# Cross-covariance attention: V and output in 2 KB runs, attention doubled by a selector matmul, and a new order of the loop

## The chip, the cores and the metric

The kernel runs on one core of one Trainium2 chip. The metric is the device time in microseconds (us) of one execution. Most executions of a kernel agree within about a per cent. For a program on one core, a run over 1.5% above the fastest of its kernel counts as slow. The engines are PE (matmul), DVE (vector), ACT (scalar), POOL and SP (which issues the DMAs).

## The reference

Q, K and V are float32 of shape (8, 12, 512, 64): 96 heads of 512 rows and 64 columns.

```python
Q_norm = Q / (np.linalg.norm(Q, axis=-2, keepdims=True) + 1e-10)
K_norm = K / (np.linalg.norm(K, axis=-2, keepdims=True) + 1e-10)
attn = np.einsum('bhnd,bhne->bhde', Q_norm, K_norm)          # 64 x 64 per head
attn = np.exp(attn - np.max(attn, axis=-1, keepdims=True))
attn = attn / (np.sum(attn, axis=-1, keepdims=True) + 1e-10)
return np.einsum('bhnd,bhde->bhne', V, attn).astype(np.float32)
```

Attention is between columns, so the only large work is to move 3 x 12.6 MB in and 12.6 MB out.

## The kernel before

A unit `u` is four heads; there are 24. All loads give each of the 128 partitions four consecutive rows of a head, so one contiguous run in memory is 4 x 64 x 4 B = 1 KB. The parts that matter (cuts marked):

```python
Vf = V.rearrange("b h (p t) d -> p (b h) t d", p=128)       # Q, K and out alike: 1 KB runs
...
def casts(u):       # DVE: four casts of Q and K to bf16, one of V
    ...
def grams(u):       # PE: 16 matmuls, [Q|K]^T [Q|K] of four heads
    ...
def norms(u):       # DVE: the squared norms from the grams' diagonals; POOL: power -0.5
    ...
def scale_k(u):     # DVE: kqs = gram * rk, masked
    ...
def logits(u):      # PE: kqs^T * stacked identities (needs scale_k)
    ...
def exps(u):        # ACT: exp with the scale rq, and row sums
    ...
def normalise(u):   # DVE: ab = exp / sum, written block-diagonally, two heads per 128 x 128
    ...
def vtrans(u):      # PE transposes V, ACT copies it out
    ...
def outs(u):        # PE: 8 matmuls of 128 x 128 x 128; ACT copies and reorders
    ...
for s in range(U + 2):
    ...                        # load unit s + 3, store unit s - 6
    if s < U:
        grams(s)
        norms(s)
    if 0 <= s - 1 < U:
        logits(s - 1)
        exps(s - 1)
    if s < U:
        vtrans(s)
    if s + CAST_AHEAD < U:
        casts(s + CAST_AHEAD)  # CAST_AHEAD = 1
    if 0 <= s - 1 < U:
        normalise(s - 1)
    if s < U:
        scale_k(s)
    if 0 <= s - 2 < U:
        outs(s - 2)
```

The loop is a software pipeline. The order written here is the order in which each engine executes; the trace shows it of PE, for one (`gram` at 71.00 us, `lg` 73.63, `vps` 74.54, `po` 75.39).

## Time and profile before

145.01 us, median of 3 runs (144.89 to 145.13).

| | before |
|---|---|
| profile's span | 143.1 us |
| busy: PE, DVE, ACT | 95.3, 100.9, 64.8 us |
| DMA packets of the data queue, their share of 16 engines | 50,688; 104.5% |
| mean granted clock of PE | 0.74 of full |

Lines of the page of the kernel before. The digits of `DMA` are tenths of busy share in 40 equal slices of the span, `GB/s` the rate in each; `q1` is the data queue (packets, MB, share of 16 engines' span); the last line is the chain of waits by engine. `PEld` is PE's loading of weights, `SPq` and the like are an engine's sequencer, which issues its instructions and DMAs, and `issue` is time for which the profile shows no wait.

```profile
span 143.1 us, 2715 instructions
...
PE 95.3 (67%) x864; PEld 83.7 (59%) x864; DVE 100.9 (71%) x432; ACT 64.8 (45%) x193; POOL 29.9 (21%) x39
...
DMA  4999999999999999999999999999999999999993
GB/s 133 336 353 349 348 348 351 350 348 348 348 350 348 376 370 378 368 371 384 368 372 380 372 376 379 371 380 371 375 369 369 371 382 372 382 377 386 377 322 113
...
q1 hardware_dynamic: 50688, 50.34, 104.5%
...
DMA 65%; DVE 14%; SPq 12%; PE 2%; ACT 1%; issue 1%; ACTq 0%
```

DMA is busy in every slice, its engines' time is used up (packet times that add up to 104.5% of the 16 engines' span: some packets of one engine must overlap in the records), and most of the chain of waits is DMA. No compute engine is above 71%. The kernel is bound by DMA, first at about 350 GB/s (loads alone), then at about 375 (loads and stores).

The groups (busy us and mean ns of one after the first bar; idle time just before them, and what ended it, after the second):

```profile
L84 DVE CAST vb<-vf 128x1024 bf16<-128x1024 f32 x24 | 16.7, 694 | 15.2 <-DMA vf<-in_V_dram 15.2
...
L100 DVE CUSTOM_DVE_ANT_0 scr<-gram,swap 128x128 f32<-128x128 f32 x48 | 13.7, 286 | 0.0
L100 DVE CUSTOM_DVE_ANT_0 scr<-gram,ident 128x128 f32<-128x128 f32 x48 | 13.6, 284 | 0.0
```

DVE waits for V's DMA, but never for PE ahead of the norms (`scr`): their idle time is 0.0.

One unit of the timeline (start us, us, engine, line, operation; in brackets the idle time before it and what ended it):

```profile
76.59 1.89 PE L92 MATMUL gram<-qkb 128*128 128x128 bf16 x16
77.47 0.69 DVE L84 CAST vb<-vf 128x1024 bf16<-128x1024 f32 x1 [0.60 <-DMA vf<-in_V_dram]
...
78.08 0.16 DVE L131 RECIPROCAL rinv<-esum 128x2 f32<-128x2 f32 x1
78.27 0.61 DVE L134 SCALAR_TENSOR_TENSOR ab<-ex,rinv,blocks 128x128 bf16<-128x128 f32 x2
78.80 0.60 DVE L111 SCALAR_TENSOR_TENSOR kqs<-gram,rq,blocks 128x128 f32<-128x128 f32 x2
...
79.20 1.12 PE L119 MATMUL lg<-eye,kqs 128*128 128x64 f32 x4 [0.73 <-DVE kqs L111]
79.32 0.28 DVE L100 CUSTOM_DVE_ANT_0 scr<-gram,ident 128x128 f32<-128x128 f32 x1
```

The grams of this unit start before V is even there to be cast, and end about when DVE comes to its multiplies, so that DVE runs casts, reciprocal, `ab`, `kqs` and the norms in one piece. `logits` (`lg`) run beside the norms. A unit takes about 5.55 us here, and DVE works about 4.2 of them.

### The profile page before, as it was taken

To read this page: it belongs to the slowest core of one execution; us is meant where nothing else is said; L and a number is where in the kernel's file an instruction comes from. 1 tells how busy PE (TensorE), PEld (TensorE's weight loads), DVE (VectorE), ACT (ScalarE), POOL (GpSimd) and SP (SyncE) were. 2 spreads that over 40 slices of the span, in tenths; PEclk is the share of its full clock that TensorE was granted. 3 is DMA by queue.
4 is the path that set the end of the run, shared out by engine and by line. 5 is a ranking of instruction groups with operands and counts; after the bars stand their busy time and mean duration, and the time that the engine had idled before them with its cause. 6 is when DMAs were issued, how large, how long until landed. Compare 5 with 4: busy or idle time off the path is not lost.

```text
span 143.1 us, 2715 instructions
## 1 busy us (share of the span) xinstructions
PE 95.3 (67%) x864; PEld 83.7 (59%) x864; DVE 100.9 (71%) x432; ACT 64.8 (45%) x193; POOL 29.9 (21%) x39
## 2 busy tenths in 40 slices
PE   0245879775896797686559874776795694397820
PEld 0234669664795686575557763765694683397620
DVE  0435888989888987696786886883868868767410
ACT  3003406764377644715706536437074273371840
POOL 6003302332033330311302303302022032031100
PEclk9999999999559856857975589655559559855555
DMA  4999999999999999999999999999999999999993
GB/s 133 336 353 349 348 348 351 350 348 348 348 350 348 376 370 378 368 371 384 368 372 380 372 376 379 371 380 371 375 369 369 371 382 372 382 377 386 377 322 113
DMA packets 50701, 50.49 MB, mean 353 GB/s; under 512 B 1536, under 2 KB 50688, under 8 KB 50688
## 3 DMA queue, kind: packets, MB, share of 16 engines
q1 hardware_dynamic: 50688, 50.34, 104.5%
q8 instruction: 6, 0.10, 0.3%
q14 instruction: 7, 0.06, 0.1%
HBM read 37.75 MB, written 12.58 MB: 352 GB/s over the span
## 4 chain that ended last, share of the span: by engine, by line
DMA 65%; DVE 14%; SPq 12%; PE 2%; ACT 1%; issue 1%; ACTq 0%
DMA vf<-in_V_dram 59%; DMA qf<-in_Q_dram 6%; SPq L65 5%; DVE vb L84 4%; SPq L66 4%; DVE ab L134 4%; SPq L70 3%; DVE scr L100 3%; DVE kqs L111 2%; PE lg L119 2%; ACT ex L125 1%; DVE rinv L131 1%; PE po L153 0%; ACT so L154 0%; DVE qkb L78 0%
## 5 line engine op out<-in xcount | busy, mean ns | idle before, releaser
L92 PE MATMUL gram<-qkb 128*128 128x128 bf16 x384 | 39.6, 283 | 20.0 <-DVE qkb L80 19.4
L105 POOL TENSOR_TENSOR rq<-nsq,mhalf 128x4 f32<-128x4 f32 x24 | 27.6, 1151 | 102.0 <-DVE nsq L100 102.0
L92 PEld LDWEIGHTS <-qkb 128*128 128x128 bf16 x384 | 33.8, 130 | 25.3 <-DVE qkb L80 24.6
L125 ACT ACTIVATE ex<-lg,rq 128x64 f32<-128x64 f32 x48 | 14.7, 310 | 63.2 <-PE lg L119 63.2
L119 PE MATMUL lg<-eye,kqs 128*128 128x64 f32 x96 | 22.8, 381 | 19.4 <-DVE kqs L111 19.3
L119 PEld LDWEIGHTS lg<-eye,kqs 128*128 128x128 f32 x96 | 18.8, 271 | 24.9 <-DVE kqs L111 24.9
L145 ACT COPY vt<-vps 128x512 bf16<-128x512 bf16 x48 | 25.7, 593 | 8.7 <-PE vps L143 8.7
L84 DVE CAST vb<-vf 128x1024 bf16<-128x1024 f32 x24 | 16.7, 694 | 15.2 <-DMA vf<-in_V_dram 15.2
L154 ACT COPY so<-po 128x512 f32<-128x512 f32 x48 | 26.4, 618 | 0.3 <-PE po L153 0.3
L143 PE MATMUL vps<-identb,vb 128*128 128x128 bf16 x192 | 20.9, 274 | 1.9 <-DVE vb L84 1.9
L153 PE MATMUL po<-ab,vt 128*128 128x128 bf16 x192 | 20.9, 274 | 0.6 <-DVE ab L134 0.6
L143 PEld LDWEIGHTS <-vb 128*128 128x128 bf16 x192 | 19.3, 138 | 2.2 <-DVE vb L84 2.2
L80 DVE CAST qkb<-kf 128x512 bf16<-128x512 f32 x24 | 10.2, 424 | 11.6 <-DMA kf<-in_K_dram 11.6
L153 PEld LDWEIGHTS <-vt 128*128 128x128 bf16 x192 | 17.4, 129 | 0.9 <-DVE ab L134 0.9
L134 DVE SCALAR_TENSOR_TENSOR ab<-ex,rinv,blocks 128x128 bf16<-128x128 f32 x48 | 14.7, 349 | 0.9
L111 DVE SCALAR_TENSOR_TENSOR kqs<-gram,rq,blocks 128x128 f32<-128x128 f32 x48 | 14.5, 344 | 0.0
L78 DVE CAST qkb<-qf 128x512 bf16<-128x512 f32 x24 | 10.2, 425 | 5.1 <-DMA qf<-in_Q_dram 5.1
L100 DVE CUSTOM_DVE_ANT_0 scr<-gram,swap 128x128 f32<-128x128 f32 x48 | 13.7, 286 | 0.0
L100 DVE CUSTOM_DVE_ANT_0 scr<-gram,ident 128x128 f32<-128x128 f32 x48 | 13.6, 284 | 0.0
L79 DVE CAST qkb<-qf 128x512 bf16<-128x512 f32 x24 | 10.1, 420 | 0.0
L81 DVE CAST qkb<-kf 128x512 bf16<-128x512 f32 x24 | 10.1, 419 | 0.0
L125 ACT ACTIVATION_READ_ACCUMULATOR ex<-lg,rq 128x1 f32 x48 | 9.4, 196 | 0.0
(18 smaller groups left out, 15.8 us busy)
## 6 DMA issues: line engine op xcount, KB each, us to landing
qf<-in_Q_dram SPq DMA_DIRECT2D x24, 512.0 KB, 8.3
kf<-in_K_dram SPq DMA_DIRECT2D x24, 512.0 KB, 8.4
vf<-in_V_dram SPq DMA_DIRECT2D x24, 512.0 KB, 8.4
out_dram<-so SPq DMA_DIRECT2D x24, 512.0 KB, 7.9
```

The costliest lines, as they stand in the source:

```text
L84: nc.vector.tensor_copy(w.rearrange("p t h d -> p h t d"), vf[u])
L92: nc.tensor.matmul(o, x, x, start=(t == 0), stop=(t == T - 1))
L100: nc.vector.tensor_tensor_reduce(out=scr, in0=blk, in1=m, scale=1.0, scalar=1e-20, op0=ALU.mult, op1=ALU.add, accum_out=n2[:, c, p:p + 1],)
L105: nc.gpsimd.tensor_tensor(out=r, in0=n2, in1=mhalf, op=ALU.pow)
L111: nc.vector.scalar_tensor_tensor(out=kk[:, p], in0=gram[u][:, p, 0::3, :], scalar=rq[u][:, 1, p:p + 1], in1=off_diag, op0=ALU.mult, op1=AL ...
L119: nc.tensor.matmul(l[:, p, :], kqs[u][:, p].rearrange("p a d -> p (a d)"), eye2)
L125: nc.scalar.activation(e[:, p, :], lg[u][:, p, :], AF.Exp, scale=rq[u][:, 0, p:p + 1], accum_out=s[:, p:p + 1])
L134: nc.vector.scalar_tensor_tensor(out=a[:, p], in0=e[:, p, None, :].to_broadcast([128, 2, D]), scalar=ri[:, p:p + 1], in1=on_diag, op0=ALU. ...
L143: nc.tensor.transpose(ps[:, t, :], vb[u][:, t, 2 * p:2 * p + 2, :].rearrange("p h d -> p (h d)"), identb)
L145: nc.scalar.copy(w, ps)
L153: nc.tensor.matmul(po[:, t], vt[u, p][:, t, :], ab[u][:, p].rearrange("p a d -> p (a d)"))
L154: nc.scalar.copy(s[:, 2 * p:2 * p + 2].rearrange("p h t d -> p t h d"), po)
```

## The change

The intent is that 2 KB runs for V and the output cost DMA less per byte. A partition then holds eight consecutive rows of V, 64 partitions make a head, and two heads lie side by side on the partitions. Row pairs are transposed (128 x 128: two rows of 64 columns), so the attention of a head is needed on both halves of the partitions, block-diagonally. A selector matmul (`pick`) doubles it, and two ACT copies place the blocks. The output matmuls become 64 columns wide and stand in pairs on the two column halves of PE. The order of the loop changes too.

```diff
-    Vf = V.rearrange("b h (p t) d -> p (b h) t d", p=128)
-    Of = out.rearrange("b h (p t) d -> p (b h) t d", p=128)
+    Vf = V.rearrange("b h n d -> (b h n d)").rearrange("(s p f) -> p s f", p=128, f=RV * D)
+    Of = out.rearrange("b h n d -> (b h n d)").rearrange("(s p f) -> p s f", p=128, f=RV * D)
@@ normalise
-            nc.vector.scalar_tensor_tensor(          # 128 x 128, with the block mask
-                out=a[:, p], in0=e[:, p, None, :].to_broadcast([128, 2, D]), ...
+            nc.vector.tensor_scalar_mul(a[:, p, :], e[:, p, :], ri[:, p:p + 1])     # 128 x 64
+    def doubled(u):
+        d = ps_d.tile([128, 2, PU, D], F32, name="dup")
+        for c in range(2):
+            nc.tensor.matmul(d[:, c], pick[:, c, :], at[u])
+        a = ab[u] = abuf[u % len(abuf)]
+        nc.scalar.copy(a[0:D, :, :, 0, :], d[0:D].rearrange("p c u d -> p u c d"))
+        nc.scalar.copy(a[D:, :, :, 1, :], d[D:].rearrange("p c u d -> p u c d"))
@@ outs
-                nc.tensor.matmul(po[:, t], vt[u, p][:, t, :], ab[u][:, p].rearrange("p a d -> p (a d)"))
+                for x in range(HS):
+                    nc.tensor.matmul(po[NV * x:NV * (x + 1), k, :], vt[u][:, g, t, NV * x:NV * (x + 1)],
+                        ab[u][:, h // 2, h % 2].rearrange("p a d -> p (a d)"), tile_position=(0, NV * x))
@@ the loop
-        if s < U:
-            grams(s)
-            norms(s)
         if 0 <= s - 1 < U:
             logits(s - 1)
             exps(s - 1)
         if s < U:
+            grams(s)
+            norms(s)
             vtrans(s)
 ...
         if 0 <= s - 2 < U:
             outs(s - 2)
+        if 0 <= s - 1 < U:
+            doubled(s - 1)
```

Left out: one vt copy of 1024 columns for two of 512, the constants, the pools' sizes.

More of the change, by code (lines that the diff above doesn't have):

```diff
@@ L17 @@
 PU = HU // 2
+RV = 8
+NV = 512 // RV
+HS = 128 // NV
+SV = HU // HS
+TP = RV // 2
 @with_exitstack
@@ L47 @@
     qkp = ctx.enter_context(tc.tile_pool(name="qkp", bufs=4))
-    vtp = ctx.enter_context(tc.tile_pool(name="vtp", bufs=4))
+    vtp = ctx.enter_context(tc.tile_pool(name="vtp", bufs=3))
     sop = ctx.enter_context(tc.tile_pool(name="sop", bufs=10))
@@ L52 @@
     ps_v = ctx.enter_context(tc.tile_pool(name="ps_v", bufs=2, space=bass.MemoryType.PSUM))
-    ps_l = ctx.enter_context(tc.tile_pool(name="ps_l", bufs=2, space=bass.MemoryType.PSUM))
+    ps_l = ctx.enter_context(tc.tile_pool(name="ps_l", bufs=1, space=bass.MemoryType.PSUM))
+    ps_d = ctx.enter_context(tc.tile_pool(name="ps_d", bufs=1, space=bass.MemoryType.PSUM))
     ps_o = ctx.enter_context(tc.tile_pool(name="ps_o", bufs=2, space=bass.MemoryType.PSUM))
@@ L58 @@
     STORE_LAG = 6
-    qf, kf, vf, vb, qkb, gram, nsq, kqs, rq, lg, ex, ab, vt, so = ({} for _ in range(14))
+    qf, kf, vf, vb, qkb, gram, nsq, kqs, rq, lg, ex, at, ab, vt, so = ({} for _ in range(15))
     def load_qk(u):
@@ L68, in load_v @@
     def load_v(u):
-        vf[u] = vp.tile([128, HU, T, D], F32, name="vf")
-        nc.sync.dma_start(out=vf[u], in_=Vf[:, u * HU:(u + 1) * HU])
+        vf[u] = vp.tile([128, SV, RV * D], F32, name="vf")
+        nc.sync.dma_start(out=vf[u], in_=Vf[:, u * SV:(u + 1) * SV])
     def store(u):
-        nc.sync.dma_start(out=Of[:, u * HU:(u + 1) * HU], in_=so[u])
+        nc.sync.dma_start(out=Of[:, u * SV:(u + 1) * SV], in_=so[u])
     def casts(u):
@@ L81, in casts @@
         nc.vector.tensor_copy(t_[:, 1::2, :, 0:D], kf[u][:, 1::2])
-        w = vb[u] = vbp.tile([128, T, HU, D], BF16, name="vb")
-        nc.vector.tensor_copy(w.rearrange("p t h d -> p h t d"), vf[u])
+        w = vb[u] = vbp.tile([128, SV, TP, 2 * D], BF16, name="vb")
+        nc.vector.tensor_copy(w.rearrange("p s t d -> p s (t d)"), vf[u])
     def grams(u):
@@ L131, in normalise @@
         nc.vector.reciprocal(ri, s)
-        a = ab[u] = small.tile([128, PU, 2, D], BF16, name="ab")
+        a = at[u] = small.tile([128, PU, D], BF16, name="at")
         for p in range(PU):
-            nc.vector.scalar_tensor_tensor(
-                out=a[:, p], in0=e[:, p, None, :].to_broadcast([128, 2, D]), scalar=ri[:, p:p + 1], in1=on_diag,
-                op0=ALU.mult, op1=ALU.mult,
-            )
-    def vtrans(u):
-        for p in range(PU):
-            ps = ps_v.tile([128, T, 128], BF16, name="vps")
-            for t in range(T):
-                nc.tensor.transpose(ps[:, t, :], vb[u][:, t, 2 * p:2 * p + 2, :].rearrange("p h d -> p (h d)"), identb)
-            w = vtp.tile([128, T, 128], BF16, name=f"vt{p}")
-            nc.scalar.copy(w, ps)
-            vt[u, p] = w
@@ L148, in outs @@
-    def outs(u):
-        s = so[u] = sop.tile([128, HU, T, D], F32, name="so")
-        for p in range(PU):
-            po = ps_o.tile([128, T, 2, D], F32, name="po")
-            for t in range(T):
-                nc.tensor.matmul(po[:, t], vt[u, p][:, t, :], ab[u][:, p].rearrange("p a d -> p (a d)"))
-            nc.scalar.copy(s[:, 2 * p:2 * p + 2].rearrange("p h t d -> p t h d"), po)
+            nc.vector.tensor_scalar_mul(a[:, p, :], e[:, p, :], ri[:, p:p + 1])
[6 more added lines that the diff above has]
+        nc.scalar.copy(a[D:, :, :, 1, :], d[D:].rearrange("p c u d -> p u c d"))
@@ new lines, in vtrans @@
+    def vtrans(u):
+        ps = ps_v.tile([128, SV, TP, 128], BF16, name="vps")
+        for g in range(SV):
+            for t in range(TP):
+                nc.tensor.transpose(ps[:, g, t, :], vb[u][:, g, t, :], identb)
+        w = vt[u] = vtp.tile([128, SV, TP, 128], BF16, name="vt")
+        nc.scalar.copy(w, ps)
+    def outs(u):
+        s = so[u] = sop.tile([128, SV, TP, 2 * D], F32, name="so")
+        for i in range(2):
+            po = ps_o.tile([128, 4, 2 * D], F32, name="po")
+            for k in range(4):
+                g, t = divmod(4 * i + k, TP)
+                for x in range(HS):
+                    h = g * HS + x
+                    nc.tensor.matmul(
+                        po[NV * x:NV * (x + 1), k, :], vt[u][:, g, t, NV * x:NV * (x + 1)],
+                        ab[u][:, h // 2, h % 2].rearrange("p a d -> p (a d)"), tile_position=(0, NV * x),
+                    )
+            nc.scalar.copy(s.rearrange("p g t d -> p (g t) d")[:, 4 * i:4 * i + 4, :], po)
@@ L171 @@
     nc.gpsimd.tensor_tensor(out=eye2, in0=ident[:, :D], in1=ident[:, D:], op=ALU.add)
-    blocks = const.tile([128, 3, D], F32, name="blocks")
-    nc.gpsimd.memset(blocks, 0.0)
-    nc.gpsimd.memset(blocks[0:D, 1, :], 1.0)
-    nc.gpsimd.memset(blocks[D:, 0, :], 1.0)
-    nc.gpsimd.memset(blocks[D:, 2, :], 1.0)
-    off_diag = blocks[:, 0:2, :]
-    on_diag = blocks[:, 1:3, :]
+    off_diag = const.tile([128, 2, D], F32, name="off_diag")
+    nc.gpsimd.memset(off_diag, 0.0)
+    nc.gpsimd.memset(off_diag[0:D, 1, :], 1.0)
+    nc.gpsimd.memset(off_diag[D:, 0, :], 1.0)
+    pick = const.tile([128, 2, 128], BF16, name="pick")
+    for c in range(2):
+        for i in range(2):
+            nc.gpsimd.tensor_copy(pick[:, c, i * D:(i + 1) * D], ident[:, c * D:(c + 1) * D])
+    abuf = []
+    for i in range(3):
+        a = const.tile([128, PU, 2, 2, D], BF16, name=f"ab{i}")
+        nc.gpsimd.memset(a, 0.0)
+        abuf.append(a)
     mhalf = const.tile([128, 2, PU], F32, name="mhalf")
```

## The prediction

> **What bounds the kernel now.** DMA. The page's slice rows show DMA busy above 90% in all but the end slices, at 350 to 380 GB/s; 50,688 packets take 104.5% of the 16 engines' span, so a 1 KB packet costs about 48 ns of one engine. The chain of waits is 65% DMA (vf loads 59%). No compute engine is full: DVE 100.9 us of 143.1, PE 95.3, ACT 64.8. In steady state one unit (4 heads, 2 MB) takes about 5.55 us (timeline, 69 to 83 us); DVE works about 4.2 of these.
>
> **What the change does.**
> - DMA: V and output go from 1 KB to 2 KB runs, 512 packets fewer per unit. [...]
> - DVE: two 128x128 ab multiplies (pair 0.53 us) become two 128x64 ones (estimate 0.35). Casts unchanged. About 3.95 us per unit.
> - ACT: one 1024-wide vt copy for two of 512 (about equal), plus two half-partition copies (about 0.8 us): about 3.5 us per unit, not limiting.
> - PE: output matmuls 8 to 16 per unit, plus 2 selector matmuls: 1 us more per unit.
> - Order: logits(s-1) now stands ahead of grams(s). This decides it.
>
> **Critical path.** DVE issues kqs(s-1), then at once norms(s). Before, grams(s) had run earlier, during the V cast, and norms followed without a gap (DVE idle before norms: 0.0 in the groups). Now kqs(s-1) -> logits(s-1) -> grams(s) -> norms(s) is serial: PE waits for kqs, then runs both, while DVE stands idle. [...] Lengths from the timeline:
> - kqs start to logits start 0.40; to the next matmul 0.53 at full clock (29.0 us), 0.91 at half (14.9 us); 16 grams 1.18 or 1.89; to DVE about 0.1
> - norms to casts 0.92; casts 1.36; V cast 0.61; reciprocal 0.20; multiplies 0.35, then kqs
>
> Sum: 5.65 us per unit at full clock, 6.74 at half. [...]
>
> Clock: in the trace, stretches at half clock with PE busy over about 95% are followed by full clock, those at full clock below about 57% by half. The new loop leaves PE a gap of 1.7 us per unit at full clock, 0.7 at half, so it should toggle, about half each: 6.15 us. First kqs at 14.3, 23 units, then 9 us of tail: 14.3 + 141.5 + 9 = 165; profile span and measured time differ by about 2. All at full clock: 155; all at half: 180.
>
> **Predicted: 165 us, 155 to 175; faster 0.03, same 0.04, slower 0.93.**
>
> **What would show it.** DMA share falls to about 85%, mean GB/s to about 310. DVE idle ahead of its norms line, released by PE gram, 1.7 to 2.8 us per unit (40 to 65 in all). The chain of waits turns from DMA to DVE and PE lines. V and output packets halve and land no slower. DVE's waits for DMA nearly vanish.
>
> **What would make it wrong.** A clock that stays full or half throughout. Column-tiled output matmuls that stall PE beyond its gap (slower still). Casts or norms shorter than the timeline shows, so that DMA still bounds[...].

The sum is whole: 14.3 + 23 x 6.15 + 9 = 165. The DMA share of 85% was the estimate; the kernel before's 104.5% of 143.1 us, spread over a span of 163, would be 92%. DMA does not bound: the 5.55 us per unit of the kernel before are already under 5.65. Estimates are also the 0.35 us for the multiplies and the 0.8 for the two copies; 0.43 and 0.73 (2 x 367 ns) were measured.

## The result

The changed kernel takes 169.66 us (168.46 to 171.19, 4 runs); the ratio to the kernel before is 1.167 (95% interval 1.160 to 1.175). Ratios here and below are the mean time of one kernel's fast runs over that of the other's in the same rounds, so not quite the ratio of the quoted medians. The one exception is e9, whose recorded ratio its two fast runs alone do not give (see there).

The first profile fell in the run of 171.19 us, which counts as slow (1.6% above the fastest). Run e10 below repeats the kernel, with a profile of state fast; it shows the same pieces with the same lengths, so the reading does not rest on the state.

Lines of the page of the changed kernel, same parts as before, with the chain by line as well:

```profile
span 169.1 us, 3252 instructions
...
PE 104.8 (62%) x1104; PEld 92.3 (55%) x1104; DVE 94.4 (56%) x432; ACT 83.5 (49%) x217; POOL 33.6 (20%) x45
...
DMA  4999999999999999999999999999998113033063
GB/s 173 321 372 361 360 360 361 360 360 360 368 385 388 386 386 378 390 388 391 386 391 386 358 334 300 343 311 361 343 377 342 49 75 124 14 116 124 0 241 131
...
q1 hardware_dynamic: 38400, 50.34, 85.9%
...
DVE 45%; PE 39%; DMA 6%; issue 3%; ACT 2%; SPq 1%; ACTq 0%; DVEq 0%
PE gram L98 22%; PE lg L125 13%; DVE scr L106 12%; DVE vb L90 8%; DMA vf<-in_V_dram 6%; DVE at L140 6%; PE dup L146 5%; DVE qkb L85 4%; DVE qkb L87 4%; DVE qkb L88 4%; DVE qkb L86 4%; DVE rinv L137 1%; ACT so L172 1%; SPq L73 1%; SPq L72 1%
```

The packets fell from 50,688 to 38,400 as planned, and DMA's engines have time over (85.9%). It is busy through three quarters of the span (9 in slices 2 to 30 of 40), as loads may run up to five units ahead (`vf` has five buffers): V's last load is issued at 120.5 us and its last cast begins at 153.0. Then little is left but stores. The chain of waits is now DVE and PE, in alternation. Its groups:

```profile
L106 DVE CUSTOM_DVE_ANT_0 scr<-gram,ident 128x128 f32<-128x128 f32 x48 | 13.9, 289 | 56.3 <-PE gram L98 56.3
...
L168 PE MATMUL po<-ab,vt 128*64 128x128 bf16 x384 | 19.5, 260 | 1.2 <-ACT ab L149 1.2
...
L90 DVE CAST vb<-vf 128x1024 bf16<-128x1024 f32 x24 | 16.4, 684 | 3.2 <-DMA vf<-in_V_dram 3.2
...
L106 DVE CUSTOM_DVE_ANT_0 scr<-gram,swap 128x128 f32<-128x128 f32 x48 | 13.7, 286 | 0.0
```

The first of the norms (`scr`, mask `ident`) now finds DVE idle for 56.3 us in all, ended by PE's grams; in the kernel before that was 0.0. In turn DVE's wait for V fell from 15.2 to 3.2 us.

The chain in order of time, one unit whose `lg` and grams ran at full clock and a part of one at half (start us, us, what; the repeated `scr` and the casts of Q and K are left out):

```profile
71.00 0.28 PE dup L146 x2
...
71.34 0.63 PE lg L125 x4
71.97 0.91 PE gram L98 x16
...
72.91 0.29 DVE scr L106
...
75.18 0.60 DVE vb L90
...
75.89 0.43 DVE at L140 x2
...
76.37 0.40 PE dup L146 x2
76.76 1.04 PE lg L125 x4
77.80 1.72 PE gram L98 x16
...
79.55 0.29 DVE scr L106
```

At 71.00 and again at 76.37 DVE's multiplies (`at`) release the doubling (`dup`); `kqs`, which follows `at` on DVE, releases `lg`, then come the grams, and only then DVE's `scr`. From `scr` to `scr` it is 6.64 us; that unit ran at half clock through `lg` (1.04) and grams (1.72). In the one before they took 0.63 and 0.91. (PE's granted clock is either full or half in the records of these traces, 1.0 or 0.5 in all 14 of the kernel before and all 34 of this one, nothing between; "at half clock" below is said of the stretch in question.) Over the whole trace, `kqs` starts first at 14.2 us and for the 24th time at 159.6: 23 units of 6.32 us in the mean (the shortest 5.37, eleven of them 6.64 or 6.65). Before, it was 14.5 to 133.2, 5.16 each. The heads and tails differ little (9.5 us after the last `kqs`, 9.9 before), so the 26 us of longer span are in the units: 23 x 1.16 = 26.7.

The work in a unit, in stretches of one unit each (columns as in the first line; the last three are clock, DMA share and GB/s). A unit at half clock of the kernel before:

```profile
core 0: us, PE busy (x) PEld busy (x) DVE busy (x) ACT busy (x) POOL busy (x), PEclk, DMA share, GB/s
...
77.80:83.40 5.60, 4.76 (x40) 4.23 (x38) 4.29 (x19) 2.64 (x8) 1.09 (x1) 0.50 1.08 373
```

Two units of the changed kernel. The first had full clock for `lg` and the grams and half clock later (0.71 in the mean), the second half clock throughout:

```profile
70.50:75.90 5.40, 3.65 (x46) 3.07 (x46) 3.89 (x19) 3.43 (x9) 1.21 (x1) 0.71 1.07 386
75.90:82.50 6.60, 4.99 (x46) 4.37 (x46) 3.88 (x18) 3.43 (x9) 1.21 (x1) 0.50 1.07 388
```

DVE works less than before (3.89 against 4.29 us), ACT more (3.43 against 2.64), PE a quarter of a microsecond more. None fills its unit. The time went into waiting.

### The profile page after: what moved, and what is told of

Read it like the earlier page. It is cut to its first block, busy times and chain, and to the rows that moved or that the text cites. A ratio compares the mean times of both kernels' runs of the same rounds, so it can differ in the third digit from the quotient of the medians.

```text
span 169.1 us, 3252 instructions
## 1 busy us (share of the span) xinstructions
PE 104.8 (62%) x1104; PEld 92.3 (55%) x1104; DVE 94.4 (56%) x432; ACT 83.5 (49%) x217; POOL 33.6 (20%) x45
## 2 busy tenths in 40 slices
DMA packets 38415, 50.53 MB, mean 299 GB/s; under 512 B 1536, under 2 KB 26112, under 8 KB 38400
## 3 DMA queue, kind: packets, MB, share of 16 engines
q1 hardware_dynamic: 38400, 50.34, 85.9%
## 4 chain that ended last, share of the span: by engine, by line
DVE 45%; PE 39%; DMA 6%; issue 3%; ACT 2%; SPq 1%; ACTq 0%; DVEq 0%
PE gram L98 22%; PE lg L125 13%; DVE scr L106 12%; DVE vb L90 8%; DMA vf<-in_V_dram 6%; DVE at L140 6%; PE dup L146 5%; DVE qkb L85 4%; DVE qkb L87 4%; DVE qkb L88 4%; DVE qkb L86 4%; DVE rinv L137 1%; ACT so L172 1%; SPq L73 1%; SPq L72 1%
## 5 line engine op out<-in xcount | busy, mean ns | idle before, releaser
L158 ACT COPY vt<-vps 128x1024 bf16<-128x1024 bf16 x24 | 24.3, 1012 | 46.9 <-PE vps L156 44.9
L106 DVE CUSTOM_DVE_ANT_0 scr<-gram,ident 128x128 f32<-128x128 f32 x48 | 13.9, 289 | 56.3 <-PE gram L98 56.3
L98 PEld LDWEIGHTS <-qkb 128*128 128x128 bf16 x384 | 41.0, 148 | 6.3 <-DVE qkb L87 6.3
L146 PE MATMUL dup<-at,pick 128*128 128x128 bf16 x48 | 7.7, 249 | 45.2 <-DVE at L140 45.1
L148 ACT CAST ab<-dup 64x256 bf16<-64x256 f32 x24 | 8.8, 367 | 24.1 <-PE dup L146 24.1
L168 PE MATMUL po<-ab,vt 128*64 128x128 bf16 x384 | 19.5, 260 | 1.2 <-ACT ab L149 1.2
L168 PEld LDWEIGHTS <-vt 128*64 128x64 bf16 x384 | 15.1, 134 | 4.8 <-issue 3.8
L117 DVE SCALAR_TENSOR_TENSOR kqs<-gram,rq,off_diag 128x128 f32<-128x128 f32 x48 | 14.5, 344 | 0.7 <-POOL rq L111 0.7
L85 DVE CAST qkb<-qf 128x512 bf16<-128x512 f32 x24 | 10.7, 445 | 4.4 <-DMA qf<-in_Q_dram 4.4
L87 DVE CAST qkb<-kf 128x512 bf16<-128x512 f32 x24 | 10.0, 418 | 0.9 <-DMA kf<-in_K_dram 0.9
L140 DVE TENSOR_SCALAR at<-ex,rinv 128x64 bf16<-128x64 f32 x48 | 10.0, 251 | 0.9
```

The lines of the kernel that those rows point to most:

```text
L85: nc.vector.tensor_copy(t_[:, 0::2, :, 0:D], qf[u][:, 0::2])
L98: nc.tensor.matmul(o, x, x, start=(t == 0), stop=(t == T - 1))
L106: nc.vector.tensor_tensor_reduce(out=scr, in0=blk, in1=m, scale=1.0, scalar=1e-20, op0=ALU.mult, op1=ALU.add, accum_out=n2[:, c, p:p + 1],)
L140: nc.vector.tensor_scalar_mul(a[:, p, :], e[:, p, :], ri[:, p:p + 1])
L146: nc.tensor.matmul(d[:, c], pick[:, c, :], at[u])
L158: nc.scalar.copy(w, ps)
```

## The experiments

The theory: the new order makes `kqs(s-1)` -> `logits(s-1)` -> `grams(s)` -> `norms(s)` a serial link between DVE and PE, and the loop through it (5.37 to 6.65 us in the trace) is mostly longer than DMA's 5.4 us (2.10 MB of a unit at the 387 GB/s that e4 shows). The rival: the added work (doubling, twice the output matmuls, ACT copies) costs the time. A third question is the clock, which the link's length follows (at full and half clock `lg` took 0.63 and 1.04 us, the grams 0.91 and 1.72). The 5.3 us of DMA per unit in the expectations is the estimate; the traces give the same, 5.55 of the kernel before less the 0.24 that e4's expectation takes from the packet records. Four kernels of the first set, e1 to e4, ran on one chip beside the kernel before (144.44 us there); e5 to e8 together (144.64); e9 and e10 together (144.91).

| run | what | median us | ratio to before (95%) |
|---|---|---|---|
| e1 | changed, old order of grams and logits | 142.56 | 0.987 (0.979 to 0.994) |
| e2 | before, new order alone | 175.49 | 1.209 (1.200 to 1.219) |
| e3 | changed, old order, doubling a unit later | 141.82 | 0.979 (0.973 to 0.985) |
| e4 | before, 2 KB runs alone (wrong result) | 140.74 | 0.971 (0.965 to 0.977) |
| e5 | changed, DVE's norms behind the casts | 144.45 | 0.999 (0.996 to 1.002) |
| e6 | changed, PE kept busy | 154.21 | 1.063 (1.057 to 1.068) |
| e7 | e3, tail split over two engines | 141.38 | 0.977 (0.974 to 0.980) |
| e8 | e3 again | 141.30 | 0.978 (0.975 to 0.981) |
| e9 | changed, doubling a unit later alone | 167.99 (fast runs 166.6) | 1.160 (1.149 to 1.171) |
| e10 | changed, again | 172.20 | 1.188 (1.184 to 1.193) |

All but e4 gave a correct result.

### e1: the old order back

```diff
+        if s < U:
+            grams(s)
+            norms(s)
         if 0 <= s - 1 < U:
             logits(s - 1)
             exps(s - 1)
         if s < U:
-            grams(s)
-            norms(s)
             vtrans(s)
```

> The changed kernel with one thing undone: grams and norms of unit s again stand ahead of logits and exps of unit s-1. Order theory (the order makes a serial loop over DVE and PE): the link through logits (0.63 us at full clock, 1.04 at half, by the changed kernel's chain) leaves the loop; but the doubling of unit s-1, which waits for the multiplies late in the DVE's unit, still stands ahead of the next grams, so a part of the loop stays: DVE work 3.95 plus idle 0.9 to 1.8 us, 4.9 to 5.75 us per unit, near the 5.3 us of DMA. Expected 142 to 150 us. Rival (cost theory: the new selector matmuls, 384 instead of 192 output matmuls and the two more ScalarE copies cost the time, the order does not matter): stays at 162 or more.

Measured 142.56 us: with all the added work in place, the loss is gone. The rival falls, and with it the smaller pools of the change, which this kernel has too. The waits of this kernel (what waited for what: us in total, times, longest):

```profile
DVE scr L106 <- PE gram L98: 26.1, 22, 1.7
```

The idle time ahead of the norms has halved, not vanished: the doubling still holds the grams until the multiplies are done. The units are 4.68 us at full clock and 5.60 at half. That is near DMA's pace of 5.4 us, so little of it shows in the total.

### e2: the new order alone

```diff
-        if s < U:
-            grams(s)
-            norms(s)
         if 0 <= s - 1 < U:
             logits(s - 1)
             exps(s - 1)
         if s < U:
+            grams(s)
+            norms(s)
             vtrans(s)
```
(in the kernel before; nothing else is changed)

> The kernel before with the changed order alone (logits and exps of unit s-1 ahead of grams and norms of unit s), nothing else. Order theory: DVE work 4.2 us per unit plus idle ahead of the norms of about 1.4 (full clock) or 2.6 us (half), 5.5 to 6.8 us per unit, in all 160 to 172 us, DVE idle ahead of norms 35 to 60 us. Cost theory: about 145 us, as before.

Measured 175.49 us, above the stated range: the order alone costs more than the whole change. The idle time ahead of the norms is the changed kernel's:

```profile
PE lg L119 <- DVE kqs L111: 60.7, 24, 3.8
DVE scr L100 <- PE gram L92: 56.3, 23, 2.7
```

Two engines wait for each other in turn. Why it went over the range: its units run from 5.55 to 6.78 us, as stated, but 14 of the 23 are over 6.7, the half-clock length. I had counted on a more even mix. The clock records of this trace (from 17 us to the last `kqs`) give full clock for 37% of the time, but for only 11% of the time of `lg` and the grams; e10 shows why.

### e3: old order, and the doubling one unit later

```diff
 # on top of e1
+        if 0 <= s - 2 < U:
+            doubled(s - 2)
         if s < U:
             vtrans(s)
 ...
             outs(s - 2)
-        if 0 <= s - 1 < U:
-            doubled(s - 1)
```

> The changed kernel with the old order and the doubling one unit later (of unit s-2, after logits of s-1, so that it waits for nothing). Order theory: no PE wait is left between kqs and norms, DVE idle ahead of norms near 0, DMA bounds again at about 5.3 us per unit: 138 to 142 us, faster than the kernel before. Cost theory: 160 or more.

Measured 141.82 us, as stated. Its data queue and chain by engine:

```profile
q1 hardware_dynamic: 38400, 50.34, 101.4%
...
DMA 72%; DVE 9%; SPq 8%; ACT 3%; PE 3%; issue 1%; ACTq 0%
```

The wait of DVE for the grams in the same kernel (engine, line and tile, what it waited for: us in total, times, longest us):

```profile
DVE scr L106 <- PE gram L98: 1.0, 1, 1.0
```

DMA bounds again, with the fewer packets. This version beats both kernels, by about 2% against the kernel before.

### e4: the 2 KB runs alone

```diff
-    Vf = V.rearrange("b h (p t) d -> p (b h) t d", p=128)
-    Of = out.rearrange("b h (p t) d -> p (b h) t d", p=128)
+    Vf = V.rearrange("b h n d -> (b h n d)").rearrange("(s p f) -> p s f", p=128, f=8 * D)
+    Of = out.rearrange("b h n d -> (b h n d)").rearrange("(s p f) -> p s f", p=128, f=8 * D)
```
(in the kernel before, with the two transfers reshaped to match; the matmuls take the rows for others than they are)

> The kernel before with V read and the output written in 2 KB runs and nothing else changed; the result is wrong on purpose (rows land where the matmuls do not expect them). It measures what the 2 KB runs are worth where DMA bounds. From the traces: a 2 KB packet took 84 ns (median) where two of 1 KB took 92, so about 0.24 us per unit, 6 us in all: 138 to 141 us. If the packets' length is worth nothing because the memory bounds: 145.

Measured 140.74 us, 3.7 us less than the kernel before beside it by the medians (3.3 to 5.0 by the ratio's interval). So this is what the longer runs are worth by themselves. Rates by slice, and the queue:

```profile
GB/s 125 334 358 360 363 363 364 355 358 362 363 363 357 389 382 383 382 382 391 387 382 394 386 383 393 384 387 388 389 377 392 383 396 383 386 404 407 335 310 159
...
q1 hardware_dynamic: 38400, 50.34, 102.5%
```

Against the page of the kernel before, loads alone rise from about 350 to 360 GB/s, loads with stores from about 375 to 387. e3 with all the real work comes within 1.1 us of this.

### e5: the same PE order, another place for the norms on DVE

```diff
             grams(s)
-            norms(s)
             vtrans(s)
         if s + CAST_AHEAD < U:
             casts(s + CAST_AHEAD)
+        if s < U:
+            norms(s)
```

> The changed kernel, PE order left as it is, but on DVE the norms of unit s now stand behind the casts of unit s+1. Order theory in full (the time is lost only because DVE's very next instruction behind kqs waits for the PE link): the casts, about 1.95 us, fill the wait; the loop is kqs 0.53 + casts 1.95 (or the PE link, 2.1 to 3.3) + norms 0.84 + the POOL power 1.4 = 4.8 to 5.6 us per unit, near the 5.3 of DMA: 140 to 148 us, DVE idle ahead of norms under 20 us in all. Rival (logits ahead of grams costs PE itself the time, whatever DVE does): 162 or more.

Measured 144.45 us. PE's order is the changed kernel's, and 25 us are gone because DVE has the casts to do while PE runs the link:

```profile
DVE kqs L117 <- POOL rq L111: 18.0, 24, 1.2
...
DVE scr L106 <- PE gram L98: 7.6, 9, 2.7
```

DVE's wait for PE fell from 56.3 to 7.6 us, and a smaller one for POOL's power came in its place, 18.0 us. Neither the order on PE nor that on DVE loses the time by itself: it takes a link on PE and a DVE whose next instruction in order waits for that link.

### e6: PE kept busy in its gap

```diff
         d = ps_d.tile([128, 2, PU, D], F32, name="dup")
+        for _ in range(12):
+            nc.tensor.matmul(d[:, 0].rearrange("p u d -> p (u d)"), pick[:, 0, :], pick[:, 1, :])
         for c in range(2):
             nc.tensor.matmul(d[:, c], pick[:, c, :], at[u])
```

> The changed kernel with 12 useless 128-column matmuls ahead of each doubling, in the time in which PE waits for the multiplies (1.65 us or more per unit in the changed kernel's trace); the result is unchanged. Clock theory (the loop runs at 5.37 us per unit at full clock and at 6.64 at half, and is mostly at half because PE idles in it): [...] units 5.4 us, 14.2 + 23 x 5.4 + 9.5 + 2 = 150 us (147 to 155). Rival (the clock makes little difference, or the filler only delays): 168 or more.

Measured 154.21 us: 288 useless matmuls make the changed kernel some 15 us faster. The units are 5.37 us where the clock is full (13 of 23 within 0.02 of it), their mean 5.61. PE was busy for 67% of such a unit (3.58 of 5.37 us); in the changed kernel's one unit wholly at full clock it was 53% (2.82 of 5.37). The changed kernel's PE gaps of over 0.5 us (from 18 us to the last `kqs`) were 2.0 us in the mean, 2.6 at most; here the useless matmuls take 0.84 us of a unit at full clock and leave a gap of 1.7. From 18 us to the last `kqs` the records give full clock for 78% of the time, and for 68% of that of `lg` and the grams. The wait for the grams shrank accordingly:

```profile
DVE scr L106 <- PE gram L98: 40.0, 23, 2.7
```

Of the changed kernel's 25 us of loss, about 15 fell away with the clock (the changed kernel did not run beside this one, so the 15 is rough). The other 10 are the link at full clock, and the units that still ran slower.

### e7 and e8: a shorter tail

```diff
 # e7, on top of e3: for the last two units
+        if u >= U - 2:
+            nc.vector.tensor_copy(a[D:, :, :, 1, :], ...)   # one of the two doubling copies on DVE
+            if u >= U - 2 and i == 0:
+                nc.vector.tensor_copy(o, po)                # one of the two output copies on DVE
```

> The kernel of e3 with, in the last two units, one of the two doubling copies and one of the two output copies on DVE, which idles there. e3's chain ends 4.1 us of ScalarE and PE work after the last multiplies; about 1 us of it would fall away: 140.5 to 142 us, at most 0.7% under e3. If the end is bound by the stores' drain instead: as e3.

> e3 unchanged, beside e7 on the same chip with more rounds: a ratio of 0.975 to 0.985 to the kernel before. It tells whether e3 is faster by over 2% and whether e7 gains anything.

e8 repeats e3: 141.30 us, ratio 0.978 (0.975 to 0.981). e7's 141.38 and 0.977 are not distinct from it: inconclusive, and no gain can be claimed. Whether e3 is faster by over 2% is at the edge of the interval.

### e9: the doubling a unit later, logits still first

```diff
 # in the changed kernel
             grams(s)
             norms(s)
+        if 0 <= s - 2 < U:
+            doubled(s - 2)
+        if s < U:
             vtrans(s)
 ...
-        if 0 <= s - 1 < U:
-            doubled(s - 1)
```

> The changed kernel, logits still ahead of grams, but the doubling one unit later as in e3: the fourth corner beside the changed kernel, e1 and e3. Order theory: the link kqs - logits - grams - norms stays whole; only the doubling's 0.1 us between kqs and logits falls away, so 2 to 3 us less than the changed kernel: 164 to 169 us, DVE idle ahead of norms still over 45 us. Rival (the doubling's wait for the multiplies is what holds PE up, and e1 gained by chance of the two together): under 155.

Measured 167.99 us (the two fast runs 166.34 and 166.79). With the changed kernel (172.20 beside it), e1 and e3 this is the fourth corner. The recorded ratio of 1.160 seems to count the slow runs too: the mean of the two fast ones, 166.6, is 1.150 times that of the kernel before beside them. Fast runs against fast runs, moving the doubling is worth 5.5 us where logits stand first (2 to 3 were expected; 166.6 against 172.1) and about 1 where they do not (142.0 against 142.9); moving the logits is worth 25 us with the doubling late and 29 without, across two sessions. The rival of this run falls. The doubling's own part is small: the shortest and longest units are 5.34 and 6.58 us (5.37 and 6.64 in the changed kernel), 1.4 us at most in 23 units. The rest of the gain is that more units had full clock for their link (mean 6.07 us against 6.40 in e10).

### e10: the changed kernel again

> The changed kernel once more, beside e9 on the same chip, for a profile in the fast state (the first profile fell in a run 1.6% above the fastest). 168 to 171 us; units of 5.4 us at full clock and 6.64 at half, as in the first profile; if the slower run had another cause, the lengths of its pieces would differ from this one's.

Measured 172.20 us, just over the stated range, on another chip than e1 to e8. The profile is of a fast run of 172.05 us. PE's clock by slice, as the page has it, and the chain by engine:

```profile
PEclk9999999999999998769678555555769678587965
...
DVE 45%; PE 41%; DMA 6%; issue 2%; SPq 1%; ACT 1%; POOLq 1%; ACTq 0%; DVEq 0%
```

Its wait of DVE for the grams:

```profile
DVE scr L106 <- PE gram L98: 58.2, 23, 2.7
```

The same waits, the same pieces: its units are 6.64 us in 15 of 23, the shortest full ones 5.6. It is slower than the first profile's 171.19 because fewer units caught the full clock (mean 6.40 against 6.32), with no piece longer. In its first 15 slices the page prints a clock of 9 where the units take the half-clock 6.64 us, with the 1.65 us of idle PE that goes with half clock throughout; the trace has no clock record before 63 us there. The mean granted clock of a run (0.807 here, 0.735 in the first profile) is therefore no measure of it; the lengths of the units are.

What decides which units are caught can be read from the clock records of the traces. They change in steps of 3.41 us, so a half and a full stretch in turn last 6.83 us, and a unit 6.64. Six units in a row of the first profile (from 38.5 us) show what follows:

| half stretch begins, us after the unit's `kqs` | 0.14 | 0.33 | 0.52 | 0.73 | 1.12 | 1.89 |
|---|---|---|---|---|---|---|
| length of the unit, us | 6.64 | 6.64 | 6.62 | 6.43 | 6.06 | 5.37 |

A half stretch that begins with the link covers `lg` and the grams, and the full stretch behind it is spent largely on PE's gap. It begins 0.19 us later after each unit of 6.64 us, and more after the shorter ones, until it misses the link and a unit is short. e10 repeats this row (0.29, 0.48, 0.66, 1.01, 1.66 us; 6.64, 6.64, 6.48, 6.17, 5.58). In e9, whose longest units are 6.58, it begins 0.25 us later after each of them and is through sooner. Between such rows stand up to three units wholly at half clock (in e10, by their lengths, more before 63 us); how many, and where a run starts in this cycle, I did not settle.

## Why the prediction was right

165 us (155 to 175) was predicted, 169.66 measured.

- **DMA bound before, no longer after**: right. The queue's share fell to 85.9% (85% predicted). The mean rate was 299 GB/s (310 predicted). The loss isn't spread as the text suggested: DMA is busy at first, running ahead, and idle at the end.
- **The gain in DMA**: it is 3.7 us in e4 by medians and 4.1 by means. The median packet took 46 ns at 1 KB and 84 at 2 KB in the packet records of the traces, so two short ones cost 9% more than a long one.
- **The order decides**: right, and shown from both sides. The order alone in the kernel before gives the loss (e2), taking it back removes it (e1), and giving DVE other work in the link does too (e5). PE ran its matmuls in the written order in the chain: grams whose data had long been cast waited 0.63 to 1.04 us behind `lg`.
- **The loop's length, 5.65 and 6.74 us**: measured 5.37 and 6.64. At full clock DVE's gap was 1.45 us (2.72 at half), against 1.7 and 2.8.
- **DVE idle ahead of the norms 40 to 65 us**: 56.3. **DVE 3.95 us of work per unit**: 3.89. **ACT about 3.5**: 3.43. **DVE's waits for DMA nearly vanish**: from 31.9 us (vf, kf, qf) to 8.5.
- **"V and output packets ... land no slower"**: wrong for V, whose median from issue to landing went from 8.4 to 9.3 us (output 7.9 to 8.0); Q and K went up as well, and in e3 and e4, which are faster, V took 9.4. The time from issue to landing is no measure of the pace here.
- **The step that was off: "it should toggle, about half each: 6.15 us"**. The mean was 6.32 (6.40 in e10). Counting from 5.37 and 6.64, the units lay only a quarter of the way to full clock: (6.64 - 6.32) / 1.27. The clock did toggle: its records in the first profile, from 18 us to the last `kqs`, give full clock for 42% of the time. But `lg` and the grams had it for only 12% of theirs, because the half stretches kept step with the units (e10). So the share of time was nearly right, and to take it for the share of units was wrong. Luck hid a part of this: the two lengths had been put too high, and with the measured ones half each would have been 6.0, not 6.15.
- **The clock rule, 95% and 57%**: it does come out of the clock records of the kernel before, in stretches of 3.41 us from 25 us on. Half clock went to full behind stretches with PE busy 95% or more (six) and stayed behind 92% or less (ten); full went to half behind 55% or less (seven) and stayed behind 59% or more (six). It is a count from that trace, not a rule for others. The changed kernel's first profile is near it (half went to full behind 94% or more, sixteen; full went to half behind 62% or less, seventeen), but in e10 half went to full behind 82%, and in e6 full stayed behind 50%.
- **PE's work and gap**: "output matmuls 8 to 16 per unit ...: 1 us more per unit", and from it "a gap of ... 0.7 at half", were mis-sized. The 16 column-tiled matmuls of the changed kernel took 1.06 us at half clock, as long as the 8 before. Here is that group in the timeline of the kernel before:

```profile
80.97 1.06 PE L153 MATMUL po<-ab,vt 128*128 128x128 bf16 x8
```

and in that of the changed kernel, with its weight loads:

```profile
80.29 0.82 PEld L168 LDWEIGHTS <-vt 128*64 128x64 bf16 x16 [0.20 <-issue]
80.29 1.06 PE L168 MATMUL po<-ab,vt 128*64 128x128 bf16 x16
```

So PE's gap in a unit wholly at half clock was 1.65 us, not 0.7. What this added to the loss is not separated from the rest. The 0.20 us ahead of the first weight load is ended by nothing that the profile shows; 0.19 also stands ahead of the weight loads of `lg`, so it is not shown to come from the 64 columns.
- **The sum**: in the profiled run (171.19 us) the longer mean unit is 23 x (6.32 - 6.15) = 3.9 us of the 6.2 over the prediction. Another 2.1 is a slip: 14.3 + 141.5 + 9 is a span, and the 2 us by which the measured time is longer were named and not added (the bounds of 155 and 180 have them).

The chances were right: the loss is over 2%, and by far.

## What to carry to other kernels

In a software pipeline over engines that each work in order, look at the point where one engine's next instruction needs another engine's answer to its last one: whatever stands between the two on the other engine becomes serial (here `lg` and the grams, for which DVE stood idle 56.3 us). Put work that is ready (here grams whose data was cast a unit earlier; e1 took 142.56 us) ahead of work that waits, or hand an engine other work after it has released a neighbour (e5, 144.45 us). A DMA gain shows only if the compute loop stays under the new, shorter DMA time, so compare the loop's length after the change, link by link, with that (here 6.32 us in the mean against 5.4). And where PE idles in each turn, do not take the full clock for granted: read the clock records for the matmuls in the loop (here `lg` and the grams had half clock for 88% of their time).
